# A hybrid attention and convolution trunk on one core: every 1/sqrt moved from VectorE to one GpSimd power instruction

## The chip, the cores and the metric

The kernel runs on one core of a Trainium2 chip. A core has five engines that run side by side, each with its own queue: TensorE (matmuls and transposes, written PE in the profile, with its weight loads as PEld), VectorE (DVE), ScalarE (ACT), GpSimd (POOL) and SyncE (SP, which here only issues DMAs). An instruction starts when it is first in its engine's queue and the semaphores that it waits for have arrived. The metric is the time of one execution on the device in microseconds; for the kernel before it is the median of three runs. One more execution was recorded by the profiler.

## The reference, cut to what matters

Four layers run one after the other on x of 512 tokens by 1024 channels, float32. Layers 0 and 3 are a differential attention (A), layer 1 is a convolution module (B), layer 2 is a latent attention (C). Each begins with an RMS norm and adds its result to x. All that the change touches is the factor 1/sqrt in the norms:

```
def _rms_norm(x, g):
    y = x * lax.rsqrt(jnp.mean(x * x, axis=-1, keepdims=True) + NORM_EPS)
    return y * g
# A: q, k of 8 heads x 2 halves x 64: _rms_norm, then rotary; per head
#    p0 - lam * p1 of two softmaxes, times v; _rms_norm(o, sub_g); * silu(gate); @ w_out
# B: u = a * sigmoid(b); causal depthwise convolution of 31 taps; LayerNorm; silu; * silu(gate); @ w_out
# C: low-rank q and kv, _rms_norm of each latent, of q's and k's parts per head; softmax; * silu(gate); @ w_out
```

## The kernel before, in words

Every float32 matrix product is made of three faster ones: each operand is split into a high part (a cast, mostly on ScalarE) and a low part (a subtraction, on VectorE, in layer 1 on GpSimd). Weights come by DMA in pieces of 256 rows by up to 512 columns (`piece`) into the `raw` buffers (three) and are split into the `w` buffers (four). Activations stand with channels on partitions as X, with Hh and Hl as the split, gain-scaled input of the next layer.

The kernel isn't written in the order in which it runs. A planner (`Plan`) collects every operation as a node with an engine, a cost in microseconds, its readers and writers. `order` then plays the engines against each other with these costs: at each step every engine offers the node that could start first, ties being broken by a priority (the order of writing plus a shift from the table SHIFT, one entry per name and engine), and the node that starts first overall is put next. So the table of shifts and the costs set the order of every engine's queue; the instructions' real durations don't change it. Buffers come from small pools (SLOTS), among them one PSUM buffer `o` in which each head's output is summed.

`rsqrt(v, name)` (line 715) is called at these places:
- `norm_end` (line 864), once per layer, four times: sums of squares of X (made on GpSimd in `norm_block`, tile `L_sqs`) go through a small matmul to `L_ss`, then to the variance `L_v`; the result scales later what the layer's first matmuls gave. Four columns.
- `qk_chunk` in `layer_a` (line 997), four times in layers 0 and 3: 32 columns, result `L_qk_y`.
- `attend_` in `layer_a` (line 1057), once per head, eight times in layers 0 and 3: four columns, result `L_h_or_y`, with which `gate_o` scales the head's output from `o` into V.
- `layer_b`, once: the LayerNorm after the convolution (line 1287), four columns, result `L_lnr_y`, then eight VectorE instructions normalise V, which TensorE transposes (`L_ytr`).
- `layer_c`, once per token tile (three columns, `L_c_y`), and in `q_chunk` (16 columns, `L_q_y`) and `kv_chunk` (8 columns, `L_kv_y`) four times each.

The ten instructions are one group: an integer estimate of the result from the bits of v, then three rounds of Newton's iteration with three instructions each. Nothing of another node comes between them on VectorE. They need a second buffer `_t`.

In layer 1 the convolution is divided: four channel blocks on VectorE (tile `L_c`), two as sums on GpSimd of products that ScalarE makes (`L_cq`, `L_ct`), one on TensorE. The rest of GpSimd's work is the weight splits of layer 1 (`L_ab_w`, `L_g_w`, `L_o_w`), three of layer 0, and the sums of squares.

Of the kernel before, what the change touches and what calls it, by code (L numbers as in the profile page):

```python
# [207 lines left out]
L0_h1_p.dve=1045 L0_h1_sc.dve=265 L0_h1_sc.pe=-311 L0_h1_wt.act=-4 L0_h1_wtr.pe=-292 L0_h2_cf.dve=448
L0_h2_mx.dve=-1387 L0_h2_or_y.dve=2129 L0_h2_osq.act=-1195 L0_h2_oss.dve=-8105 L0_h2_ov.dve=-485 L0_h2_p.act=579
L0_h2_p.dve=-5549 L0_h2_sc.dve=2135 L0_h2_sc.pe=-157 L0_h2_wt.act=-6662 L0_h2_wtr.pe=8 L0_h3_cf.dve=1197  # L210
L0_h3_mx.dve=-11983 L0_h3_or_y.dve=2 L0_h3_osq.act=139 L0_h3_oss.dve=-245 L0_h3_p.act=-4374 L0_h3_p.dve=-517
L0_h3_sc.dve=-1955 L0_h3_sc.pe=1655 L0_h3_wt.act=43 L0_h3_wtr.pe=-193 L0_h4_cf.dve=-1967 L0_h4_mx.dve=4
# [50 lines left out]
L1_yv3.act=365 L1_yv3.dve=1128 L1_yv4.act=-161 L1_yv4.dve=1380 L1_yv5.act=608 L1_yv5.dve=-6 L1_yv6.dve=687
L1_yv7.act=45 L1_yv7.dve=-1903 L2_T.dve=-208 L2_c00_sq.act=23 L2_c00_t.dve=314 L2_c00_y.dve=-1770 L2_c01_sq.act=22
L2_c01_t.dve=-360 L2_c01_v.dve=13054 L2_c01_y.dve=5452 L2_c02_sq.act=3689 L2_c02_t.dve=-1714 L2_c02_v.dve=18723
L2_c02_y.dve=6901 L2_c03_sq.act=-2 L2_c03_t.dve=2 L2_c03_y.dve=-198 L2_c0_a.pe=2275 L2_c0_w.act=2065 L2_c0_w.dve=-447
# [1301 lines left out]
```

## Time and profile before

| | |
|---|---|
| median of 3 runs | 1075.49 us (1072.21 to 1076.08) |
| the profiled execution | 1068.59 us |
| its span, first to last instruction | 1066.7 us |
| TensorE busy | 1012.0 us (95%) |
| VectorE busy | 806.8 us (76%), 2271 instructions |
| ScalarE busy | 642.1 us (60%) |
| GpSimd busy | 209.2 us (20%), 133 instructions |
| mean granted TensorE clock | 0.986 of full speed |

Busy shares overlap, since the engines run side by side. TensorE's matmuls are pipelined and their ends are modelled, so that its busy time is not time at full rate. What counts for the end is where TensorE stands still or another engine is on the chain of work that ended last; an engine that is idle elsewhere costs nothing.

### The profile page before, as it was taken

To read this page: it belongs to the slowest core of one execution; us is meant where nothing else is said; L and a number is where in the kernel's file an instruction comes from. 1 tells how busy PE (TensorE), PEld (TensorE's weight loads), DVE (VectorE), ACT (ScalarE), POOL (GpSimd) and SP (SyncE) were. 2 spreads that over 40 slices of the span, in tenths; PEclk is the share of its full clock that TensorE was granted. 3 is DMA by queue.
4 is the path that set the end of the run, shared out by engine and by line. 5 is a ranking of instruction groups with operands and counts; after the bars stand their busy time and mean duration, and the time that the engine had idled before them with its cause. 6 is when DMAs were issued, how large, how long until landed. Compare 5 with 4: busy or idle time off the path is not lost.

```text
span 1066.7 us, 15176 instructions
## 1 busy us (share of the span) xinstructions
PE 1012.0 (95%) x5089; PEld 840.0 (79%) x5089; DVE 806.8 (76%) x2271; ACT 642.1 (60%) x1351; POOL 209.2 (20%) x133
## 2 busy tenths in 40 slices
PE   7999999998999999995999998999999999999798
PEld 6778877886887887774888777888888788888687
DVE  4764999997755999999256769976573699988871
ACT  6466458658744356895343676754423957667862
POOL 3300000000038599993330000001020000000000
PEclk9999999999999999997999999999999999999899
DMA  8223121220114331302122211112333212312002
GB/s 235 80 70 108 60 80 60 80 83 22 40 41 139 99 99 40 111 17 65 55 94 65 85 49 40 42 36 81 102 95 119 75 58 67 99 40 80 21 21 79
DMA packets 67253, 78.15 MB, mean 73 GB/s; under 512 B 15813, under 2 KB 44741, under 8 KB 67176
## 3 DMA queue, kind: packets, MB, share of 16 engines
q1 hardware_dynamic: 67176, 77.19, 23.8%
q8 instruction: 40, 0.66, 0.3%
q14 instruction: 37, 0.30, 0.1%
HBM read 75.08 MB, written 2.10 MB: 72 GB/s over the span
## 4 chain that ended last, share of the span: by engine, by line
PE 60%; DVE 16%; ACT 12%; issue 5%; POOL 5%; DMA 1%; SPq 1%; DVEq 0%; ACTq 0%; POOLq 0%
PE L_o L451 18%; PE L_g_a L451 12%; PE L_qk_a L451 10%; PE L_v_a L451 6%; ACT L_qk_st L488 3%; DVE L_c L513 3%; POOL L_cq L504 3%; PE L_ab_a L451 2%; POOL L_sqs L504 1%; PE L_c_a L451 1%; ACT G L481 1%; PE L_ytr L457 1%; DVE L_qk_T L501 1%; DVE L_qk_st L501 1%; SPq L545 1%
## 5 line engine op out<-in xcount | busy, mean ns | idle before, releaser
L451 PE MATMUL L_qk_a<-L_qk_w,Hh 128*128 128x512 f32 x512 | 163.0, 399 | 0.5 <-ACT Hh L481 0.5
L451 PE MATMUL L_o<-L_y,L_o_w 128*128 128x512 f32 x576 | 142.5, 398 | 3.0 <-ACT L_y L481 1.7
L504 POOL TENSOR_TENSOR L_sqs<-L_sqs,L_sq 128x512 f32<-128x512 f32 x28 | 43.8, 1564 | 497.3 <-ACT L_sqs L481 264.7
L451 PEld LDWEIGHTS L_o<-L_y,L_o_w 128*128 128x128 f32 x576 | 106.6, 190 | 25.7 <-DVE L_y L513 2.1
L451 PE MATMUL L_g_a<-L_g_w,Hh 128*128 128x512 f32 x384 | 120.1, 394 | 0.3 <-ACT V L481 0.3
L451 PEld LDWEIGHTS L_qk_a<-L_qk_w,Hh 128*128 128x128 f32 x512 | 93.7, 190 | 18.2 <-ACT Hh L481 0.7
L513 DVE SCALAR_TENSOR_TENSOR L_c<-L_u,L_tab,L_c 128x512 f32<-128x512 f32 x150 | 104.2, 743 | 1.0
L451 PE MATMUL L_qk_a<-L_qk_w,Hl 128*128 128x512 f32 x256 | 101.0, 394 | 3.8 <-DVE Hl L513 3.8
L451 PEld LDWEIGHTS L_g_a<-L_g_w,Hh 128*128 128x128 f32 x384 | 70.5, 188 | 15.0 <-ACT V L481 0.9
L451 PE MATMUL L_v_a<-L_v_w,Hh 128*128 128x512 f32 x256 | 81.2, 398 | 0.2 <-ACT V L481 0.2
L451 PE MATMUL L_ab_a<-Hh,L_ab_w 128*128 128x512 f32 x256 | 81.3, 393 | 0.1
L504 POOL TENSOR_TENSOR L_cq<-L_cq,L_ct 128x512 f32<-128x512 f32 x60 | 79.6, 1327 | 5.5 <-ACT L_ct L481 2.1
L451 PE MATMUL L_g_a<-L_g_w,Hl 128*128 128x512 f32 x192 | 75.0, 390 | 0.0
L451 PEld LDWEIGHTS L_qk_a<-L_qk_w,Hl 128*128 128x128 f32 x256 | 48.4, 189 | 15.1 <-DVE Hl L513 4.6
L488 ACT CAST L_qk_st<-L_qk_tr 64x512 fp32r<-64x512 f32 x96 | 55.6, 579 | 4.8 <-PE L_qk_tr L457 3.7
L451 PEld LDWEIGHTS L_ab_a<-Hh,L_ab_w 128*128 128x128 f32 x256 | 48.0, 188 | 11.4 <-DVE L_u L501 1.1
L488 ACT CAST L_g_w<-L_g_w_r 128x1024 fp32r<-128x1024 f32 x32 | 33.6, 1053 | 36.9 <-PE L_v_a L451 23.3
L501 DVE TENSOR_TENSOR L_qk_st<-L_qk_tr,L_qk_st 64x512 fp32r<-64x512 f32 x64 | 44.1, 688 | 15.2 <-ACT L_qk_st L488 13.9
L481 ACT ACTIVATE L_ct<-L_u,L_tab 128x512 f32<-128x512 f32 x60 | 43.2, 721 | 19.8 <-POOL L_cq L504 19.3
L451 PEld LDWEIGHTS L_v_a<-L_v_w,Hh 128*128 128x128 f32 x256 | 46.0, 188 | 9.1 <-ACT V L481 0.4
L501 DVE TENSOR_TENSOR L_qk_w<-L_qk_w_r,L_qk_w 128x1024 fp32r<-128x1024 f32 (+1 forms) x30 | 35.4, 1182 | 22.0 <-ACT L_qk_w L488 21.6
L488 ACT CAST L_qk_w<-L_qk_w_r 128x1024 fp32r<-128x1024 f32 (+1 forms) x33 | 34.0, 1032 | 28.6 <-PE L_g_a L451 18.6
(377 smaller groups left out, 2373.1 us busy)
## 6 DMA issues: line engine op xcount, KB each, us to landing
L_qk_w_r<-a_w_in SPq DMA_DIRECT2D x62, 256.0 KB, 3.0
L_v_w_r<-a_w_in SPq DMA_DIRECT2D x16, 512.0 KB, 4.2
L_g_w_r<-a_w_in SPq DMA_DIRECT2D x16, 512.0 KB, 3.7
L_o_w_r<-a_w_out SPq DMA_DIRECT2D x16, 512.0 KB, 3.5
L_ab_w_r<-b_w_in SPq DMA_DIRECT2D x24, 256.0 KB, 2.9
L_g_w_r<-b_w_in SPq DMA_DIRECT2D x8, 512.0 KB, 3.7
L_o_w_r<-b_w_out SPq DMA_DIRECT2D x8, 512.0 KB, 3.5
L_g_w_r<-c_w_in SPq DMA_DIRECT2D x8, 512.0 KB, 3.7
```

What stands on the lines that cost most here:

```text
L451: lambda nc: nc.tensor.matmul(out.real(), a.real(), b.real(), start=start, stop=stop),
L457: emit = lambda nc: nc.tensor.transpose(out.real(), src.real(), ident.real())
L481: nc.scalar.activation(out.real(), src.real(), func, scale=scale.real() if isinstance(scale, View) else scale, **kw)
L488: lambda nc: nc.scalar.copy(out.real(), src.real()), [src], [out])
L501: lambda nc: nc.vector.tensor_tensor(out=out.real(), in0=a.real(), in1=b.real(), op=op), [a, b], [out])
L504: lambda nc: nc.gpsimd.tensor_tensor(out=out.real(), in0=a.real(), in1=b.real(), op=op), [a, b], [out])
L513: self.add("dve", out.n / 960.0 + (0.13 if isinstance(scalar, View) else 0.068), lambda nc: nc.vector.scalar_tensor_tensor(out=out.real(), ...
L545: lambda nc: q(nc).dma_start(out.real(), src), [], [out], dma=out.n * 4 * parts)
```

## The change

`rsqrt` becomes one GpSimd instruction, v to the power of -0.5, as a tensor_tensor with a constant tile. The constant, 32 columns of -0.5, is set once by VectorE at the start. In the planner the node has a cost of 1.0 us on GpSimd at every width, in place of a VectorE group with the sum of ten instructions' costs and 1.15. The buffer `_t` goes. The table SHIFT is replaced as a whole: 875 entries before, 892 after, 770 names in common, none with the same value; entries of GpSimd are 12 before and 47 after.

```diff
 SHIFT = {k: int(v) for k, v in (x.split("=") for x in """
-L0_g0_a.act=27 L0_g0_a.pe=-118 L0_g0_w.act=560 L0_g0_w.dve=-4872 L0_g0_w_r.sp=8 L0_g1_a.act=-39309 L0_g1_a.pe=1592
...
+L3_y1.dve=-176 L3_y2.act=-5673 L3_y2.dve=-13 L3_y3.act=1884 L3_y3.dve=1217 L3_ytr0.pe=962 L3_ytr1.pe=5075
...
 """.split())}
...
         self.p.memset(self.ones[:, :], 1.0)
+        self.p.memset(self.half[:, :], -0.5)
...
     def rsqrt(self, v, name):
 
-        p = self.p
-        y, t = self.small(v.n, name + "_y"), self.small(v.n, name + "_t")
-        with p.group("dve"):
-            p.ts(y.bitcast(I32), v.bitcast(I32), -0.5, ALU.mult, 1597463007.0, ALU.add)
-            for _ in range(3):
-                p.stt(t, y, -0.5, y, ALU.mult, ALU.mult)
-                p.tt(t, t, v, ALU.mult)
-                p.stt(y, t, 1.5, y, ALU.add, ALU.mult)
-            p.open.cost += 1.15
+        y = self.small(v.n, name + "_y")
+        h = self.half[:, 0:v.n]
+        self.p.add("pool", 1.0, lambda nc: nc.gpsimd.tensor_tensor(
+            out=y.real(), in0=v.real(), in1=h.real(), op=ALU.pow), [v, h], [y])
         return y
...
-    for n, shape, dt in (("ident", [P, P], F32), ("ones", [P, P], F32), ("X", [P, NK, S], F32),
+    for n, shape, dt in (("ident", [P, P], F32), ("ones", [P, P], F32), ("half", [P, 32], F32), ("X", [P, NK, S], F32),
```

## Rows read from the trace of the kernel before

**Rows 1.** The page: busy time by engine; GpSimd's busy tenths in 40 slices.
```profile
PE 1012.0 (95%) x5089; PEld 840.0 (79%) x5089; DVE 806.8 (76%) x2271; ACT 642.1 (60%) x1351; POOL 209.2 (20%) x133
...
POOL 3300000000038599993330000001020000000000
```

**Rows 2.** The page: the chain that ended last, by engine.
```profile
PE 60%; DVE 16%; ACT 12%; issue 5%; POOL 5%; DMA 1%; SPq 1%; DVEq 0%; ACTq 0%; POOLq 0%
```

**Rows 3.** Stretches: length, busy PE, PEld, DVE, ACT, POOL; granted clock, DMA share, GB/s.
```profile
120.00:180.00 60.00, 59.34 (x301) 47.99 (x300) 56.08 (x154) 37.23 (x77) 0.00 (x0) 1.00 0.23 69
...
240.00:300.00 60.00, 54.24 (x300) 44.49 (x299) 44.23 (x173) 44.00 (x115) 0.00 (x0) 0.97 0.09 28
...
480.00:505.00 25.00, 12.13 (x60) 9.44 (x59) 24.49 (x56) 13.04 (x22) 8.54 (x5) 0.73 0.21 69
...
590.00:640.00 50.00, 47.40 (x241) 39.60 (x239) 39.02 (x132) 35.55 (x77) 0.00 (x0) 1.00 0.21 61
640.00:700.00 60.00, 52.80 (x352) 47.66 (x352) 56.20 (x216) 40.50 (x115) 0.00 (x0) 0.97 0.14 45
...
985.00:1030.00 45.00, 37.51 (x201) 30.76 (x200) 37.61 (x149) 34.80 (x84) 0.00 (x0) 0.92 0.04 13
```

**Rows 4.** TensorE's waits: waiter <- releaser: us in total, times, longest.
```profile
PE L_ytr L457 <- ACT L_h5j_p L481: 4.6, 1, 4.6
...
PE L_h2j_wtr L457 <- ACT L_h2j_p L481: 2.6, 1, 2.6
```

**Rows 5.** Timeline 484 to 506: start, us, engine, line, operation [idle before <-releaser].
```profile
484.88 1.31 POOL L504 TENSOR_TENSOR L_cq<-L_cq,L_ct 128x512 f32<-128x512 f32 x1
...
486.24 1.12 PE L457 MATMUL L_ctr<-ident,L_cq 128*128 128x128 f32 x4 [5.60 <-POOL L_cq L504]
...
491.60 0.17 DVE L522 TENSOR_SCALAR L_lnr_y<-L_v 128x4 int32<-128x4 int32 x1
...
493.38 0.16 DVE L513 SCALAR_TENSOR_TENSOR L_lnr_y<-L_lnr_t,L_lnr_y 128x4 f32<-128x4 f32 x1
493.57 3.74 DVE L522 TENSOR_SCALAR V<-V,L_mv,L_lnr_y 128x512 f32<-128x512 f32 x8
...
494.27 4.67 PE L457 MATMUL L_ytr<-ident,V 128*128 128x128 f32 x20 [6.91 <-DVE V L522]
```

**Rows 6.** Timeline of VectorE, 988 to 991: one chain of 32 columns.
```profile
988.54 0.18 DVE L522 TENSOR_SCALAR L_qk_y<-L_qk_v 128x32 int32<-128x32 int32 x1
...
990.56 0.19 DVE L513 SCALAR_TENSOR_TENSOR L_qk_y<-L_qk_t,L_qk_y 128x32 f32<-128x32 f32 x1
```

**Rows 7.** Line 522: count, ns min/median/max, first and last start in us.
```profile
L522 DVE TENSOR_SCALAR L_r_y<-L_v x4: 160/170/1174, 50.4 to 791.5; 128x4 int32<-128x4 int32 x4
...
L522 DVE TENSOR_SCALAR L_kv_y<-L_kv_v x4: 164/168/173, 599.1 to 692.3; 128x8 int32<-128x8 int32 x4
...
L522 DVE TENSOR_SCALAR L_q_y<-L_q_v x4: 166/168/175, 605.6 to 685.9; 128x16 int32<-128x16 int32 x4
```

**Rows 8.** Line 504, GpSimd: the same columns.
```profile
L504 POOL TENSOR_TENSOR L_cq<-L_cq,L_ct x60: 1260/1296/1782, 367.9 to 484.9; 128x512 f32<-128x512 f32 x60
L504 POOL TENSOR_TENSOR L_sqs<-L_sqs,L_sq x28: 1272/1460/2158, 23.4 to 779.2; 128x512 f32<-128x512 f32 x28
...
L504 POOL TENSOR_TENSOR L_o_w<-L_o_w_r,L_o_w x8: 2377/2410/2864, 475.2 to 530.2; 128x1024 fp32r<-128x1024 f32 x8
```

**Rows 9.** Layer 2's tables: line 501 by form, and the chain: start, us, what.
```profile
L501 DVE TENSOR_TENSOR L_tab<-L_setup x18: 277/348/2565, 21.0 to 709.7; 128x128 f32<-128x128 f32 x12, 128x256 f32<-128x256 f32 x6
...
481.98 7.25 DVE L_tab L501 x6
```

**Rows 10.** Stretch 240 to 300, records of the tile L_h_or_t alone: VectorE.
```profile
240.00:300.00 60.00, 5.84 (x36) 0.97 0.09 28
```

**Rows 11.** The chain of waits, 625 to 705: start, us, what.
```profile
654.05 0.19 DVE L_q_y L522
...
658.70 0.47 ACT L_h2j_p L481 x2
```

More of the change, by code (lines that the diff above doesn't have):

```diff
@@ L208 @@
[L208 to L212, printed above, removed]
@@ L263 @@
[L263 to L266, printed above, removed]
-L2_c0_w_r.sp=-5670 L2_g0_a.pe=24924 L2_g0_w.act=-506 L2_g0_w.dve=130 L2_g0_w_r.sp=2796 L2_g1_a.act=1554 L2_g1_a.pe=392
@@ L338 @@
-L3_ytr2.pe=-50 L3_ytr3.pe=-23 L3_ytr4.pe=-2546 L3_ytr5.pe=-630 L3_ytr7.pe=-46 none.act=3426 none.dve=28
+L0_g0_a.act=-3563 L0_g0_a.pe=-1240 L0_g0_w.act=6679 L0_g0_w.dve=-45 L0_g1_a.act=-17044 L0_g1_a.pe=-2 L0_g1_w.act=-2673
+L0_g1_w.dve=4891 L0_h0_cf.dve=196 L0_h0_mx.dve=62 L0_h0_or_y.dve=280 L0_h0_or_y.pool=231 L0_h0_osq.act=8822
+L0_h0_oss.dve=310 L0_h0_ov.dve=-265 L0_h0_p.act=2958 L0_h0_p.dve=214 L0_h0_sc.dve=-217 L0_h0_sc.pe=-1938
+L0_h0_wt.act=-2027 L0_h0_wtr.pe=3135 L0_h1_cf.dve=-231 L0_h1_mx.dve=144 L0_h1_or_y.dve=183 L0_h1_or_y.pool=-1633
@@ new lines @@
+L0_h1_osq.act=1884 L0_h1_oss.dve=5505 L0_h1_ov.dve=-23927 L0_h1_p.act=-2142 L0_h1_p.dve=199 L0_h1_sc.dve=-7
+L0_h1_sc.pe=1482 L0_h1_wtr.pe=-15202 L0_h2_cf.dve=-28 L0_h2_mx.dve=-6468 L0_h2_or_y.dve=7565 L0_h2_osq.act=951
+L0_h2_oss.dve=-4299 L0_h2_ov.dve=2637 L0_h2_p.act=-44448 L0_h2_p.dve=-1247 L0_h2_sc.dve=-26647 L0_h2_sc.pe=-4
+L0_h2_wt.act=-3852 L0_h3_mx.dve=1362 L0_h3_or_y.dve=-297 L0_h3_or_y.pool=-31 L0_h3_osq.act=-4253 L0_h3_ov.dve=819
+L0_h3_p.act=15 L0_h3_p.dve=176 L0_h3_sc.dve=1377 L0_h3_sc.pe=-2546 L0_h3_wt.act=-153 L0_h3_wtr.pe=111
@@ new lines @@
+L0_h6_wt.act=-5174 L0_h6_wtr.pe=-1442 L0_h7_cf.dve=1069 L0_h7_mx.dve=-1 L0_h7_or_y.dve=1186 L0_h7_or_y.pool=-3223
+L0_h7_osq.act=2070 L0_h7_oss.dve=-245 L0_h7_ov.dve=553 L0_h7_p.act=-1465 L0_h7_p.dve=159 L0_h7_sc.dve=-2
+L0_h7_sc.pe=-12 L0_h7_wt.act=102 L0_h7_wtr.pe=-137 L0_lay.act=2013 L0_lay.dve=-7848 L0_o0.pe=-1804 L0_o01.dve=1392
+L0_o01.pe=77 L0_o02.dve=-17861 L0_o02.pe=-811 L0_o03.dve=2420 L0_o03.pe=-75 L0_o0_w.act=14 L0_o0_w.dve=2975
+L0_o0_w_r.sp=-3322 L0_o1.dve=1763 L0_o1.pe=-9320 L0_o10.dve=4099 L0_o10.pe=321 L0_o11.dve=-7541 L0_o11.pe=182
@@ new lines @@
+L0_qk1_st.act=3336 L0_qk1_st.dve=-3316 L0_qk1_t.dve=1 L0_qk1_tr.pe=-1811 L0_qk1_v.dve=2079 L0_qk1_w.act=3870
+L0_qk1_w.dve=-2062 L0_qk1_y.dve=-31 L0_qk2_a.pe=244 L0_qk2_sq.act=619 L0_qk2_ss.dve=-4813 L0_qk2_st.act=4574
+L0_qk2_st.dve=-5 L0_qk2_t.dve=2 L0_qk2_tr.pe=-15 L0_qk2_v.dve=4789 L0_qk2_w.act=14287 L0_qk2_y.dve=-999
+L0_qk2_y.pool=7478 L0_qk3_T.dve=-2835 L0_qk3_a.pe=1002 L0_qk3_sq.act=-6762 L0_qk3_ss.dve=741 L0_qk3_st.act=188
+L0_qk3_st.dve=-1103 L0_qk3_t.dve=307 L0_qk3_tr.pe=-2509 L0_qk3_v.dve=-20325 L0_qk3_w.act=274 L0_qk3_w.dve=-10607
@@ new lines @@
+L0_tr20.act=15 L0_tr20.dve=-2286 L0_tr20.pe=3080 L0_tr24.act=-1196 L0_tr24.dve=-2238 L0_tr24.pe=1472 L0_tr30.act=288
+L0_tr30.dve=-1451 L0_tr30.pe=-405 L0_tr34.act=2592 L0_tr34.dve=332 L0_tr34.pe=280 L0_v.dve=-18577 L0_v0_a.act=45
+L0_v0_a.pe=-4828 L0_v0_w.act=1353 L0_v0_w.dve=-4216 L0_v0_w_r.sp=-285 L0_v1_a.act=-1282 L0_v1_a.pe=1076
+L0_v1_w.act=2766 L0_v1_w.dve=2736 L0_v1_w_r.sp=2657 L0_warm.pe=-7816 L0_x1.sp=492 L0_y0.act=-4856 L0_y0.dve=-225
+L0_y1.act=1684 L0_y1.dve=-6296 L0_y2.act=264 L0_y2.dve=-163 L0_y3.act=1390 L0_y3.dve=2806 L0_ytr1.pe=457
@@ new lines @@
+L1_yv1.dve=-1646 L1_yv2.act=478 L1_yv2.dve=-153 L1_yv3.act=-683 L1_yv3.dve=-5059 L1_yv4.act=-77 L1_yv5.act=5963
+L1_yv5.dve=-1091 L1_yv6.act=-1192 L1_yv6.dve=-2338 L1_yv7.act=-1942 L1_yv7.dve=273 L2_T.act=8677 L2_T.dve=224
+L2_c00_sq.act=89 L2_c00_t.dve=-1284 L2_c00_v.dve=-3125 L2_c00_y.dve=-683 L2_c00_y.pool=8218 L2_c01_sq.act=-718
+L2_c01_t.dve=245 L2_c01_v.dve=17 L2_c01_y.dve=793 L2_c01_y.pool=1042 L2_c02_sq.act=-7 L2_c02_t.dve=1545
+L2_c02_v.dve=-11316 L2_c02_y.dve=-12069 L2_c02_y.pool=135 L2_c03_sq.act=7020 L2_c03_t.dve=-11509 L2_c03_y.dve=571
@@ new lines @@
+L2_c03_y.pool=472 L2_c0_a.pe=-4 L2_c0_w_r.sp=-4750 L2_g0_a.act=-919 L2_g0_a.pe=182 L2_g0_w.act=1011 L2_g0_w.dve=-74
+L2_g0_w_r.sp=-785 L2_g1_a.act=1771 L2_g1_a.pe=-14467 L2_g1_w.act=2348 L2_g1_w.dve=1888 L2_g1_w_r.sp=2643
+L2_h0_mx.dve=167 L2_h0_p.act=883 L2_h0_wt.act=-1115 L2_h0_wtr.pe=-8758 L2_h1_mx.dve=-953 L2_h1_p.act=-1344
+L2_h1_sc.dve=-22 L2_h1_sc.pe=-1333 L2_h1_wt.act=-46 L2_h1_wtr.pe=-12873 L2_h2_mx.dve=-1800 L2_h2_p.act=-5336
+L2_h2_sc.dve=-47 L2_h2_sc.pe=-5910 L2_h2_wt.act=647 L2_h2_wtr.pe=-10004 L2_h3_mx.dve=-1027 L2_h3_p.act=-5
@@ new lines @@
+L2_h3_sc.dve=77 L2_h3_wtr.pe=-458 L2_h4_mx.dve=-4016 L2_h4_p.act=-1430 L2_h4_sc.pe=-623 L2_h4_wt.act=-922
+L2_h4_wtr.pe=-3946 L2_h5_mx.dve=6 L2_h5_p.act=1316 L2_h5_sc.dve=21 L2_h5_sc.pe=-1673 L2_h5_wt.act=1398
+L2_h5_wtr.pe=1475 L2_h6_mx.dve=3095 L2_h6_p.act=3976 L2_h6_sc.dve=-90 L2_h6_sc.pe=-6207 L2_h6_wt.act=-11388
+L2_h6_wtr.pe=-4991 L2_h7_mx.dve=-134 L2_h7_sc.pe=-1185 L2_h7_wt.act=-936 L2_h7_wtr.pe=-209 L2_kv0_T.act=1339
+L2_kv0_T.dve=111 L2_kv0_a.pe=1490 L2_kv0_sq.act=47 L2_kv0_ss.dve=-862 L2_kv0_v.dve=263 L2_kv0_w.act=-4388
@@ new lines @@
+L2_kv0_w.dve=4586 L2_kv0_w_r.sp=11972 L2_kv1_T.act=831 L2_kv1_T.dve=-1882 L2_kv1_a.act=3472 L2_kv1_a.pe=-2007
+L2_kv1_sq.act=582 L2_kv1_ss.dve=4408 L2_kv1_v.dve=701 L2_kv1_w.dve=125 L2_kv1_w_r.sp=4593 L2_kv1_y.pool=9931
+L2_kv2_T.act=-296 L2_kv2_T.dve=716 L2_kv2_a.act=-4922 L2_kv2_a.pe=1100 L2_kv2_sq.act=-2025 L2_kv2_ss.dve=-2820
+L2_kv2_v.dve=-38 L2_kv2_w.act=-572 L2_kv2_w.dve=2040 L2_kv3_T.act=249 L2_kv3_a.act=5509 L2_kv3_a.pe=4
+L2_kv3_sq.act=25406 L2_kv3_ss.dve=-206 L2_kv3_v.dve=470 L2_kv3_w.act=-31 L2_kv3_w.dve=-23904 L2_kv3_w_r.sp=-3
@@ new lines @@
+L2_kv3_y.pool=-4120 L2_l0.dve=1411 L2_l1.dve=7061 L2_l2.dve=1 L2_l3.dve=276 L2_l4.dve=303 L2_l5.dve=42134
+L2_l6.dve=-680 L2_l7.dve=555 L2_lat0.act=-2838 L2_lat1.dve=-8529 L2_lay.act=6960 L2_lay.dve=82 L2_lay.sp=-207
+L2_ltr0.pe=2471 L2_ltr1.pe=824 L2_ltr2.pe=11684 L2_ltr3.pe=-2709 L2_o0.dve=-217 L2_o0.pe=260 L2_o00.dve=-4
+L2_o00.pe=324 L2_o01.dve=-57 L2_o01.pe=131 L2_o02.dve=-46 L2_o02.pe=-1644 L2_o03.dve=54 L2_o03.pe=-451 L2_o0_w.act=-4
+L2_o0_w.dve=-1542 L2_o0_w_r.sp=1125 L2_o1.dve=3493 L2_o1.pe=588 L2_o10.pe=-56 L2_o11.dve=2123 L2_o11.pe=-5220
@@ new lines @@
+L2_o12.pe=-427 L2_o13.dve=-1335 L2_o13.pe=6482 L2_o1_w_r.sp=1027 L2_o2.dve=2500 L2_o3.dve=-4931 L2_o3.pe=-15596
+L2_o4.dve=2906 L2_o4.pe=44053 L2_o5.dve=362 L2_o5.pe=-15 L2_o6.dve=-1056 L2_o6.pe=-1783 L2_o7.dve=-8440 L2_o7.pe=214
+L2_p0_rt.act=-4348 L2_p0_rt.dve=-16 L2_p0_rtr.pe=-5764 L2_p0_st.act=14084 L2_p0_tr.pe=2 L2_p1_rt.act=75
+L2_p1_rt.dve=-645 L2_p1_rtr.pe=21 L2_p1_st.act=-278 L2_p1_st.dve=5679 L2_p1_tr.pe=-21 L2_p2_rt.act=-9
+L2_p2_rt.dve=13965 L2_p2_rtr.pe=289 L2_p2_st.act=-57 L2_p2_st.dve=-3776 L2_p2_tr.pe=1823 L2_p3_rt.act=-17355
@@ new lines @@
+L3_h7_or_y.dve=-1201 L3_h7_or_y.pool=1502 L3_h7_osq.act=-3 L3_h7_oss.dve=-1757 L3_h7_ov.dve=6404 L3_h7_p.act=118
+L3_h7_p.dve=11809 L3_h7_sc.dve=-1361 L3_h7_wt.act=-2249 L3_h7_wtr.pe=1521 L3_lay.act=1348 L3_lay.dve=-3889
+L3_lay.sp=1396 L3_o0.dve=-4885 L3_o00.pe=-204 L3_o01.pe=3093 L3_o02.pe=2413 L3_o03.pe=977 L3_o0_w.act=163
+L3_o0_w.dve=987 L3_o0_w_r.sp=-19724 L3_o1.dve=-1373 L3_o1.pe=123 L3_o10.pe=670 L3_o11.pe=3441 L3_o12.pe=-2347
+L3_o130.pe=7734 L3_o131.pe=8550 L3_o1_w.act=4236 L3_o1_w_r.sp=17041 L3_o2.dve=971 L3_o2.pe=-1144 L3_o3.dve=886
@@ new lines @@
+L3_o4.dve=-269 L3_o4.pe=-14 L3_o5.dve=-909 L3_o5.pe=4169 L3_o6.pe=66 L3_o7.dve=-13256 L3_o7.pe=-1835 L3_ot000.act=1923
+L3_ot000.sp=-2525 L3_ot010.act=15 L3_ot010.sp=2238 L3_ot020.sp=-11579 L3_ot030.act=297 L3_ot030.sp=-19755
+L3_ot100.act=15 L3_ot110.act=264 L3_ot110.sp=-43 L3_ot120.act=-2638 L3_ot120.sp=-205 L3_ot130.act=-2046
+L3_ot130.sp=1150 L3_ot13256.act=-519 L3_ot13256.sp=3066 L3_qk0_a.pe=400 L3_qk0_sq.act=-1200 L3_qk0_st.act=-23
+L3_qk0_t.dve=-889 L3_qk0_tr.pe=880 L3_qk0_v.dve=249 L3_qk0_w.act=1585 L3_qk0_w.dve=1527 L3_qk0_w_r.sp=-84
@@ new lines @@
+L3_qk3_w.act=788 L3_qk3_w.dve=10369 L3_qk3_w_r.sp=-4 L3_qk3_y.dve=-49 L3_qk3_y.pool=3280 L3_r10.dve=42
+L3_r11.dve=-1883 L3_r13.dve=-59 L3_r14.dve=77 L3_r15.dve=218 L3_r16.dve=16604 L3_r17.dve=-4153 L3_r_y.pool=1030
+L3_rq.dve=275 L3_setup.dve=-4577 L3_setup.sp=381 L3_sq1.act=3356 L3_sq2.act=-21 L3_sq4.act=14467 L3_sq5.act=111
+L3_sq6.act=1269 L3_sq7.act=47 L3_sqs.act=1753 L3_sqs.pool=4017 L3_ss.pe=2046 L3_tab.dve=-111 L3_v.dve=-448
+L3_v0_a.act=-49 L3_v0_a.pe=-1723 L3_v0_w.act=-48 L3_v0_w.dve=-35 L3_v0_w_r.sp=-841 L3_v1_a.act=-620 L3_v1_w.act=-971
@@ L339 @@
+L3_v1_w.dve=4248 L3_v1_w_r.sp=6300 L3_y0.act=-49 L3_y0.dve=13627 L3_y1.act=12395 L3_y1.dve=867 L3_y2.act=-857
+L3_y2.dve=4399 L3_y3.act=3190 L3_y3.dve=12 L3_ytr0.pe=-44 L3_ytr1.pe=489 L3_ytr2.pe=1783 L3_ytr3.pe=25 L3_ytr4.pe=-309
+L3_ytr5.pe=-4022 L3_ytr6.pe=-2057 L3_ytr7.pe=3 none.act=-1474 none.dve=1165
 """.split())}
```

188 lines of the change are left out of this document (65 added, 123 removed).

## The prediction

> **What bounds the kernel now.** I read the page's busy line first: TensorE is busy 1012.0 of 1066.7 us, VectorE 806.8, GpSimd 209.2 [rows 1]. So 54.7 us are all the idle TensorE time there is, and work that leaves VectorE pays only where TensorE waits for it. The chain of waits says that such places exist: a quarter of it runs over VectorE and ScalarE [rows 2]. The table by stretch says where. Taking TensorE's busy time from each stretch's length: 0.7 us idle in 120-180, although VectorE is busy 56.08 of 60 there; 5.8 in 240-300 (last heads of layer 0), 12.9 in 480-505 (end of layer 1's convolution, LayerNorm), 2.6 in 590-640 and 7.2 in 640-700 (attention of layer 2), 7.5 in 985-1030 (last heads of layer 3) [rows 3]. That is 36 us; the rest is the start, the end and small pieces. The list of TensorE's waits names the releasers: ScalarE's exponentials once for 4.6 us and once for 2.6 [rows 4]; in the timeline VectorE's normalised V for 6.91 and GpSimd's last convolution sum for 5.60 [rows 5].
>
> **What the change removes.** There are 41 calls of rsqrt: four norms at the layers' heads, one LayerNorm, 12 in each of the two A layers (4 query/key chunks, 8 heads), 12 in layer 2. The 25 calls of 3 or 4 columns run like the LayerNorm's: from 491.60 to 493.54, 1.94 us for ten instructions [rows 5]. The 8 calls of 32 columns run from 988.54 to 990.75, 2.21 us [rows 6]. For the 8 of 8 and 16 columns I take 2.02, between the two. VectorE loses 25 x 1.94 + 8 x 2.21 + 8 x 2.02 = 48.5 + 17.7 + 16.2 = 82.4 us of its queue, and 1.0 more where one first instruction took 1174 ns in place of 170 [rows 7]. In busy time that is 410 instructions of about 0.17 us, 70 us: 806.8 should become about 737. The memset of the constant, 32 columns once at the start, has no wait behind it; I count nothing (a short VectorE instruction is 0.16 us [rows 5]).
>
> **What it adds.** 41 GpSimd instructions. No row shows a power. Below it is bounded by GpSimd's addition: 1296 ns for 512 columns and 2410 for 1024 [rows 8] make 2.18 ns a column and 0.18 us fixed, so 0.19 us for 4 columns and 0.25 for 32. Above, I let the longest undisturbed GpSimd row stand, 2.4 us. The small ones are nearest in shape to the low end, but a power is many steps per element; I take 0.7, between the ends by ratio, and keep 0.2 to 2.4. The code's planner charges 1.0 for every width. Two handovers, VectorE to GpSimd and back, come on top: I take 0.15 together, a little over twice the 0.05 us between GpSimd's last convolution sum, ended at 486.19, and TensorE's transpose of it at 486.24 [rows 5]. So 0.85 us from variance to result in place of 1.94, bounds 0.35 and 2.55.
>
> The added wait is on VectorE: the instruction that uses the result (r times rs, or V times r) stands in its queue, and what is behind it waits too. The planner fills the gap for 1.0 us plus handovers; as long as a power takes less, VectorE stands still only where it has nothing else, as at the LayerNorm.
>
> GpSimd's slices show no work in most of layers 0, 2 and 3 [rows 1], so the heads' and chunks' powers meet an empty queue. In layer 1 they don't: eight weight splits of 2.4 us stand there from 475.2 to 530.2 [rows 8].
>
> A shared resource: VectorE and GpSimd disturb each other. A GpSimd sum of 1272 ns at best took up to 2158 [rows 8], a VectorE table product of 348 ns up to 2565 [rows 9], and the held instruction of [rows 7] belongs to the same kind. I take this at nothing on the path, since it costs VectorE at most the power's 0.7 us out of the 2.0 freed; its upper bound is 41 x 0.7 = 29 us of VectorE. The Trainium skill (SBUF — State Buffer, "Who interferes with whom") says that a VectorE instruction with two SBUF inputs and a GpSimd instruction that reads SBUF exclude each other for a whole instruction; the trace agrees, with the 2565 ns above. By that rule in its hardest form every power would take its length from VectorE, 54 of 83 us would stay freed, and the gain below would shrink in proportion, from 9 to 6 us.
>
> **What of it is on the path.**
> - 480-505: the LayerNorm's chain stands bare between V's variance and the V that TensorE waits for [rows 5]: 1.94 - 0.85 = 1.1 us.
> - 240-300: four of the chains lie here (36 records, nine to a chain [rows 10]), 7.8 us of VectorE against 5.8 us of TensorE idle, with ScalarE as busy as VectorE (44.00 against 44.23 [rows 3]). I take 2, a third.
> - 590-700: all eight q and kv chains, by their first and last starts [rows 7], 16 us of VectorE against 9.8 idle. One is plainly the cause: the q chain from 654.05 to about 656.1, then V, then the exponential at 658.70 for which TensorE waited 2.6 us [rows 4, 11]. In 640-700 VectorE (56.20) is well busier than ScalarE (40.50); I take 4.
> - 985-1030: the 4.6 us wait is ScalarE's own queue; I take 1.
> - Clock: 0.73 granted in 480-505 and 0.92 in 985-1030 [rows 3]; that is 6.75 and 3.6 us worth of full clock, TensorE dropping to the lower of its two levels after it had idled. Shorter waits give perhaps 1 back.
> - 120-240, 830-985 and the norms between layers: nothing, TensorE's own matmuls are the cover. If that cover were gone, each chain would cost its 0.85 us.
>
> Sum: 1.1 + 2 + 4 + 1 + 1 = 9 us. Next to be late are ScalarE in the attention tails and GpSimd's convolution at 486. Against the profiled execution, 1068.59 us, that gives about 1059.6; that execution is 6.9 us below the median of the three timed runs, 1075.49, so on their scale, 9 us lower, I forecast 1066.
>
> **The new table** reorders everything (892 entries, none of the 770 common names keeps its value). What such an order can gain or lose is seen at 480-494: from 475 on, weight splits of 2.4 us stand inside GpSimd's chain of sums [rows 8], and layer 2's tables stand for 7.25 us on VectorE, stretched from 348 ns each, ahead of the statistics that the LayerNorm needs [rows 9]. Nothing in the trace says where the new order puts them. I take zero for it, and plus or minus 8.
>
> **Rivals.**
> 1. *Relief and a better seam.* Forecast, and the 7 us of tables or one or two splits no longer ahead of LayerNorm, with 4 of the 6.75 us of clock back: 1066 - 7 - 4 = 1055. For: the size of that wait. Against: the seam is a matter of order, not of rsqrt.
> 2. *Hidden.* TensorE is 95% busy and ScalarE ends much of its waiting [rows 4]; VectorE just idles more: 1075, within 0.5%. For: 120-180 with VectorE full and TensorE not waiting.
> 3. *The power is dear.* VectorE is relieved of 2.03 us per call (83.4 over 41) minus what the power takes beyond the planner's 1.0. With the gain in proportion, at my upper bound of 2.4 it is 3 us (1072), at 3.0 us nil, and at 5 us 9 us are lost: 1084. It decides from 3.0 us on. Against: no GpSimd row of even 1024 columns is that long undisturbed.
> 4. *LayerNorm's power queued behind splits (slower).* Place: GpSimd's queue after 475. Each split put ahead of the power costs 2.4 us bare [rows 8], and the waits for the splits' own inputs on top. With three of them ahead, 7.2 us, another drop of the clock as dear as that in 985-1030 (3.6), and only 2 us of relief elsewhere: 7.2 + 3.6 - 2 = +8.8, some 1084. With so little relief it decides from the first split on, with all of the 8 us elsewhere from the fourth; the same length lost at another seam through the new order counts here too.
>
> **Chances.** Forecast 0.40, rival 1 0.15, rival 2 0.22, rival 3 0.08, rival 4 0.15. Half a per cent, 5.4 us, is about what a measurement of this kernel tells from no change. The forecast case spreads over 1059 to 1073 and gives 0.34 faster and 0.06 same; rival 1 is faster; rival 2 same; of 3 and 4 0.02 fall within the bound. Faster 0.49, same 0.30, slower 0.21. The forecast's own range is 1059 to 1073; to hold 8 in 10 it must reach rival 1 with some room and the two slow cases: 1048 to 1084.
>
> **What would show it.** Power rows of 0.2 to 1 us, about as long for 32 columns as for 4; VectorE near 1860 instructions and 737 us, GpSimd at 174 and about 240 us; TensorE's idle time down to about 46 us, the loss mostly in 590-700; V after the LayerNorm's variance within 1 us. It is wrong if a power takes over 2.4 us, if VectorE shows idle time that GpSimd ends in most chains, if TensorE's idle time stays, or if the largest difference lies at the end of the convolution and comes from the order.

## The result: 0.9% slower

The changed kernel takes 1082.24 us (median of 8 runs, 1081.49 to 1085.62) against 1073.24 for the kernel before beside it (8 runs, 1067.83 to 1076.08). The ratio is 1.0093, with a 95% interval of 1.0068 to 1.0118. The loss is small but clear of the noise. The forecast was 1066, 9 us under the kernel before, so even the sign was wrong. The profiled execution took 1082.88 us; its mean granted clock was 0.979 of full speed, where the one before had 0.986.

From the page of the kernel after: span, busy time by engine, GpSimd's busy tenths in 40 slices, the chain that ended last.

```profile
span 1081.0 us, 14821 instructions
...
PE 1016.5 (94%) x5089; PEld 840.3 (78%) x5089; DVE 741.7 (69%) x1862; ACT 640.5 (59%) x1351; POOL 294.3 (27%) x174
...
POOL 2410112020047499993521111100320020202000
...
PE 56%; DVE 13%; ACT 12%; POOL 10%; issue 6%; DMA 1%; SPq 1%; POOLq 0%; ACTq 0%; DVEq 0%
```

VectorE lost 65.1 us of work [rows 1], near the 70 of the forecast. But GpSimd gained 85.1, and its share of the chain that ended last doubled from 5% to 10% [rows 2]: by line, the wide powers are 3% of it, and the convolution's sums went from 3% to 5%. TensorE stands idle for 64.5 us (1081.0 - 1016.5), where it had been 54.7. The powers themselves say why. This is the line that issues them, by tile: count, ns min/median/max, first and last start, shapes.

```profile
L722 POOL TENSOR_TENSOR L_h_or_y<-L_h_ov,half x16: 1007/1007/1377, 156.5 to 1054.9; 128x4 f32<-128x4 f32 x16
...
L722 POOL TENSOR_TENSOR L_qk_y<-L_qk_v,half x8: 5427/5616/6345, 53.0 to 980.0; 128x32 f32<-128x32 f32 x8
...
L722 POOL TENSOR_TENSOR L_c_y<-L_c_v,half x4: 850/854/1713, 568.4 to 576.7; 128x3 f32<-128x3 f32 x4
L722 POOL TENSOR_TENSOR L_kv_y<-L_kv_v,half x4: 1637/1637/1639, 608.6 to 706.9; 128x8 f32<-128x8 f32 x4
L722 POOL TENSOR_TENSOR L_q_y<-L_q_v,half x4: 2900/2902/2932, 610.2 to 689.7; 128x16 f32<-128x16 f32 x4
...
L722 POOL TENSOR_TENSOR L_lnr_y<-L_v,half x1: 1027/1027/1027, 498.6 to 498.6; 128x4 f32<-128x4 f32 x1
```

The shortest times, 850, 1007, 1637, 2900 and 5427 ns for 3, 4, 8, 16 and 32 columns, lie on a line of about 0.38 us and 0.157 us a column ((5427 - 1007) / 28 = 158 ns). The plan charges 1.0 for each, which fits the narrow calls of 3 and 4 columns alone. A query/key chunk takes five and a half times its planned time, where the ten instructions on VectorE took 2.21 us [rows 6].

Who pays is in VectorE's waits for the powers: waiter, releaser, us in total, times, longest.

```profile
DVE L_qk_y L503 <- POOL L_qk_y L722: 29.0, 8, 5.3
...
DVE L_h_or_y L503 <- POOL L_h_or_y L722: 4.1, 6, 1.1
DVE L_q_y L524 <- POOL L_q_y L722: 3.7, 3, 1.9
DVE L_kv_T L503 <- POOL L_kv_y L722: 3.0, 4, 1.8
```

All eight chunks hold VectorE, 29.0 us together. Three of them reach TensorE with a long wait:

```profile
PE L_ctr L459 <- POOL L_cq L506: 8.2, 1, 8.2
PE L_qk_tr L459 <- DVE L_qk_T L503: 6.0, 2, 4.8
PE L_qk_tr L459 <- DVE L_qk_st L503: 5.2, 2, 5.0
PE L_ytr L459 <- DVE V L524: 4.1, 1, 4.1
...
PE L_v_a L453 <- DVE L_v_w L503: 2.9, 1, 2.9
```

The second, the third and the last row are new. How they come about is seen in the timeline of one chunk in layer 0 and two in layer 3 (start, us, engine, line, operation, in brackets the idle time before it and who ended it): GpSimd, VectorE and TensorE from 131 to 139, from 884 to 898, and from 976 to 992.

```profile
131.43 1.22 DVE L503 TENSOR_TENSOR L_v_w<-L_v_w_r,L_v_w 128x1024 fp32r<-128x1024 f32 x1
131.60 6.34 POOL L722 TENSOR_TENSOR L_qk_y<-L_qk_v,half 128x32 f32<-128x32 f32 x1 [73.21 <-DVE L_qk_v L524]
...
137.97 0.19 DVE L503 TENSOR_TENSOR L_qk_y<-L_qk_y,L_lay 128x32 f32<-128x32 f32 x1 [5.32 <-POOL L_qk_y L722]
...
138.84 2.24 PE L459 MATMUL L_qk_tr<-ident,L_qk_T 128*128 128x128 f32 x8 [4.80 <-DVE L_qk_T L503]
...
885.53 0.69 DVE L503 TENSOR_TENSOR L_qk_T<-L_qk_T,L_qk_t 128x512 f32<-128x512 f32 x1
885.71 5.80 POOL L722 TENSOR_TENSOR L_qk_y<-L_qk_v,half 128x32 f32<-128x32 f32 x1 [39.43 <-DVE L_qk_v L524]
...
891.54 0.19 DVE L503 TENSOR_TENSOR L_qk_y<-L_qk_y,L_lay 128x32 f32<-128x32 f32 x1 [3.89 <-POOL L_qk_y L722]
891.65 1.22 DVE L503 TENSOR_TENSOR L_v_w<-L_v_w_r,L_v_w 128x1024 fp32r<-128x1024 f32 x1
...
892.92 0.80 PE L453 MATMUL L_v_a<-L_v_w,Hh 128*128 128x512 f32 x1 [2.93 <-DVE L_v_w L503]
...
979.83 1.21 DVE L503 TENSOR_TENSOR L_g_w<-L_g_w_r,L_g_w 128x1024 fp32r<-128x1024 f32 x1
...
979.99 6.34 POOL L722 TENSOR_TENSOR L_qk_y<-L_qk_v,half 128x32 f32<-128x32 f32 x1 [22.18 <-DVE L_h5j_mx L503]
...
986.37 0.19 DVE L503 TENSOR_TENSOR L_qk_y<-L_qk_y,L_lay 128x32 f32<-128x32 f32 x1 [5.19 <-POOL L_qk_y L722]
986.59 0.68 DVE L503 TENSOR_TENSOR L_qk_st<-L_qk_tr,L_qk_st 64x512 fp32r<-64x512 f32 x1
...
989.69 1.09 PE L459 MATMUL L_qk_tr<-ident,L_qk_T 128*128 128x128 f32 x4 [4.98 <-DVE L_qk_st L503]
```

At 891.54 the multiplication by rs waits 3.89 us for the power. The weight split behind it, which has no use for the power, waits with it, and TensorE stands still for that split. At 986.37 the same befalls a `L_qk_st` of transposes made earlier. At 138.84 TensorE waits 4.80 us for what is scaled with the result itself, `L_qk_T`. Together that is 4.80 + 2.93 + 4.98 = 12.7 us.

Each of the three waits is followed by a stretch in which the granted clock fell to the lower of its two levels. Stretches of the kernel after: length, busy PE, PEld, DVE, ACT, POOL; granted clock, DMA share, GB/s.

```profile
138.80:146.00 7.20, 7.16 (x23) 5.73 (x24) 4.65 (x8) 4.50 (x8) 0.00 (x0) 0.60 0.25 75
...
889.00:897.00 8.00, 5.07 (x19) 3.97 (x18) 4.77 (x15) 0.68 (x2) 3.51 (x2) 0.69 0.36 123
897.00:900.00 3.00, 3.00 (x11) 2.40 (x11) 1.25 (x2) 2.93 (x6) 0.00 (x0) 0.69 0.00 0
...
987.00:995.00 8.00, 5.31 (x18) 4.47 (x19) 7.77 (x14) 6.87 (x12) 0.00 (x0) 0.57 0.20 64
```

In work at full clock that is 7.2 x 0.40 + 11 x 0.31 + 8 x 0.43 = 9.7 us. Part of it is counted among the waits already: near 892.0 and 987.6 the clock had fallen while TensorE still stood idle (granted clock 0.51 in 892 to 893, 0.79 in 987 to 988), for some 3.0 us, worth 1.5. So the clock took about 8.2 us from the work, and waits and clock make some 20.9 us.

### The profile page after: what moved, and what is told of

Same layout as the page of the kernel before. It is cut to its first block, busy times and chain, and to the rows that moved or that the text cites. A ratio compares the mean times of both kernels' runs of the same rounds, so it can differ in the third digit from the quotient of the medians.

```text
span 1081.0 us, 14821 instructions
## 1 busy us (share of the span) xinstructions
PE 1016.5 (94%) x5089; PEld 840.3 (78%) x5089; DVE 741.7 (69%) x1862; ACT 640.5 (59%) x1351; POOL 294.3 (27%) x174
## 4 chain that ended last, share of the span: by engine, by line
PE 56%; DVE 13%; ACT 12%; POOL 10%; issue 6%; DMA 1%; SPq 1%; POOLq 0%; ACTq 0%; DVEq 0%
PE L_o L453 17%; PE L_qk_a L453 13%; PE L_g_a L453 9%; PE L_v_a L453 5%; POOL L_cq L506 5%; POOL L_qk_y L722 3%; ACT L_qk_st L490 2%; PE L_c_a L453 2%; DVE L_c L515 1%; DVE L_qk_T L503 1%; PE L_ab_a L453 1%; ACT G L483 1%; ACT L_ct L483 1%; PE L_qk_tr L459 1%; DVE L_qk_st L503 1%
## 5 line engine op out<-in xcount | busy, mean ns | idle before, releaser
L453 PE MATMUL L_qk_a<-L_qk_w,Hh 128*128 128x512 f32 x512 | 165.6, 405 | 1.3 <-POOL L_qk_w L506 1.3
L453 PEld LDWEIGHTS L_o<-L_y,L_o_w 128*128 128x128 f32 x576 | 105.7, 188 | 23.2 <-POOL L_o_w L506 0.9
L722 POOL TENSOR_TENSOR L_qk_y<-L_qk_v,half 128x32 f32<-128x32 f32 x8 | 46.1, 5758 | 211.9 <-DVE L_qk_v L524 189.7
L722 POOL TENSOR_TENSOR L_h_or_y<-L_h_ov,half 128x4 f32<-128x4 f32 x16 | 16.6, 1040 | 245.6 <-DVE L_h_ov L524 130.4
L506 POOL TENSOR_TENSOR L_sqs<-L_sqs,L_sq 128x512 f32<-128x512 f32 x28 | 39.7, 1418 | 84.4 <-ACT L_sqs L483 56.4
L503 DVE TENSOR_TENSOR L_qk_st<-L_qk_tr,L_qk_st 64x512 fp32r<-64x512 f32 x64 | 44.1, 689 | 19.1 <-ACT L_qk_st L490 17.7
```

The costliest lines, as they stand in the source:

```text
L453: lambda nc: nc.tensor.matmul(out.real(), a.real(), b.real(), start=start, stop=stop),
L503: lambda nc: nc.vector.tensor_tensor(out=out.real(), in0=a.real(), in1=b.real(), op=op), [a, b], [out])
L506: lambda nc: nc.gpsimd.tensor_tensor(out=out.real(), in0=a.real(), in1=b.real(), op=op), [a, b], [out])
L722: self.p.add("pool", 1.0, lambda nc: nc.gpsimd.tensor_tensor(out=y.real(), in0=v.real(), in1=h.real(), op=ALU.pow), [v, h], [y])
```

## The experiments

In the expectations D is the theory that the wide powers, 5.6 us long but planned at 1.0, cost the time; O is the theory that the new order of the work costs it, whatever the powers take; T, in the two runs that name it, is the theory that a power costs only where it outlasts the matmuls that TensorE has at hand. Other letters are rivals for their own run. Times are medians; each ratio is to the kernel before, run on the same chip.

**Cheap powers in the same order.** The first of these makes the eight 32-column powers a multiplication by a constant; the second does so for all 41. The records of each engine stand in the same order as in the kernel after, but for one more short instruction that sets a constant; so they do in the two later runs that halve or repeat powers, the added powers aside.

```diff
...
-            out=y.real(), in0=v.real(), in1=h.real(), op=ALU.pow), [v, h], [y])
+            out=y.real(), in0=v.real(), in1=h.real(), op=ALU.mult if cheap else ALU.pow), [v, h], [y])
```

> The order of every queue is that of the changed kernel; only the eight powers of 32 columns become multiplications by a constant (their results are not 1/sqrt, so this part of the computation is left out). Theory D (dear power: the 32-column powers of 5.6 us hold VectorE's queue and with it TensorE's transposes, because the planner charged 1.0): GpSimd's eight instructions fall to 0.2 to 0.4 us, VectorE's 29.0 us of waiting for them to under 3, TensorE's 11.2 us of waiting before L_qk_tr to under 2, and the time by 8 to 13 us below the changed kernel: 1069 to 1074, ratio to before 0.996 to 1.001. Theory O (the new order is worse by itself, at the start and the end of the convolution): at most 3 us below the changed kernel, ratio 1.006 to 1.009.

> As e1, with all 41 powers as multiplications (no 1/sqrt is computed anywhere). Theory D: the powers of 16 and 8 columns (2.9 and 1.6 us) cost a little too, those of 3 and 4 columns (1.0 us, as the planner charges) nothing: 1 to 4 us below e1, ratio 0.992 to 0.999. Theory O: as e1, ratio 1.005 to 1.009. If the time lies clearly under the kernel before, the change would have paid with a power as cheap as an addition.

Measured: 1059.61 us (ratio 0.9872, 0.9852 to 0.9893) and 1056.22 (0.9853, 0.9829 to 0.9878). With the eight wide ones cheap, 22.6 us go and the kernel is faster than before; the other 33 are worth 3.4 more. That leaves no room for O, which allowed 3 us; D had the direction and the waits, but its 8 to 13 us were about half of the gain. From the first of these kernels, the multiplication that stands for a power:

```profile
L724 POOL TENSOR_TENSOR L_qk_y<-L_qk_v,half x8: 252/440/1169, 54.6 to 962.6; 128x32 f32<-128x32 f32 x8
```

The stretches around the three waits, in the kernel after (first three rows) and with cheap wide powers (last three):

```profile
120.00:180.00 60.00, 52.90 (x263) 43.12 (x263) 48.16 (x137) 36.66 (x84) 13.14 (x3) 0.94 0.20 62
830.00:900.00 70.00, 67.03 (x324) 55.28 (x323) 45.31 (x117) 40.52 (x82) 7.81 (x3) 0.95 0.22 68
985.00:1045.00 60.00, 51.99 (x277) 42.92 (x277) 43.70 (x135) 43.01 (x98) 4.51 (x4) 0.94 0.14 45
...
120.00:180.00 60.00, 57.98 (x299) 47.54 (x299) 55.65 (x163) 42.17 (x98) 3.80 (x4) 1.00 0.23 71
830.00:900.00 70.00, 69.49 (x340) 57.00 (x339) 51.78 (x142) 44.03 (x88) 2.64 (x3) 1.00 0.23 68
985.00:1045.00 60.00, 56.17 (x309) 45.88 (x309) 33.01 (x114) 31.83 (x84) 3.02 (x3) 1.00 0.10 32
```

VectorE has no wait for `L_qk_y` left, TensorE none for `L_qk_tr`, and the clock is full where it had dropped. The spans differ by 1081.0 - 1057.8 = 23.2 us. Of these 15.0 are TensorE's idle time (64.5 against 1057.8 - 1008.3 = 49.5) and 8.2 its busy time (1016.5 against 1008.3), the same 5089 matmuls at a mean clock of 0.979 against 0.990; the account above found 12.7 and 8.2. The 8.2 us for the convolution's sum stay, so they aren't the wide powers' doing.

**Each table with the other form.** One kernel takes the new table with the ten VectorE instructions, the other the old table with the powers (its values for the nodes that moved from VectorE to GpSimd moved with them). In the first kernel the new table's values for these nodes stand under GpSimd's name and apply to nothing, so that it isn't quite the new order.

```diff
 SHIFT = {k: int(v) for k, v in (x.split("=") for x in """
-(the kernel's own table)
+(the other kernel's table)
```

> The kernel before with the new table of priorities: ten VectorE instructions per rsqrt, no power. Theory D: the table alone isn't the loss; but it was made for other nodes, so some loss is possible: 1070 to 1080, ratio 0.997 to 1.006. Theory O: at least as slow as the changed kernel: 1080 to 1095, ratio 1.006 to 1.02.

> The changed kernel with the old table (each rsqrt node, now on GpSimd, keeps the old shift of its name). Theory D: the powers are as long here, VectorE waits about 25 to 35 us for the 32-column ones, and the time is 1078 to 1095, ratio 1.005 to 1.02. Theory O: with the old order the loss goes: 1065 to 1075, ratio 0.993 to 1.002.

Measured: 1183.50 us (1.1028, 1.1002 to 1.1054) and 1125.62 (1.0485, 1.0460 to 1.0511). Both are far above what either theory gave. In the second, VectorE still waits 23.9 us for the wide powers; but before against after had made a difference of 9 us, and this one of 52. So a table is worth something only with the costs that it was made for, and a swap of tables can't separate the two parts of this change. In the first, TensorE stands idle for 114.5 us (1182.0 - 1067.5) at a mean clock of 0.942, spread over many waits of which the longest is 6.8 us; no single cause is shown.

**Half as wide.** 16 of the 32 columns by power, the rest by multiplication; same order, same planned cost.

```diff
...
+            nc.gpsimd.tensor_tensor(out=y[:, 0:w].real(), in0=v[:, 0:w].real(), in1=g[:, 0:w].real(), op=ALU.pow)
+            if w < v.n:
+                nc.gpsimd.tensor_tensor(out=y[:, w:32].real(), in0=v[:, w:32].real(), in1=g[:, 32:48].real(), op=ALU.mult)
```

> The changed kernel's order again; of each 32-column power only 16 columns are a power, the others a multiplication by a constant (half of these results are not 1/sqrt). The wide call should take 2.9 + 0.3 = 3.2 us, between e1's 0.4 and the changed kernel's 5.6. Theory D in its plain form, each us beyond the planner's 1.0 has the same price: (3.2 - 0.4) / (5.6 - 0.4) = 54% of the way from 1059.6 to 1082.2: 1071 to 1073, ratio to before 0.997 to 1.000. Theory T (a threshold: TensorE has matmuls for some us, and stalls, with its clock dropping, only when the power outlasts them): under a quarter of the way, 1060 to 1065, ratio 0.987 to 0.992.

Measured: 1068.15 us (0.9974, 0.9958 to 0.9990), 8.5 above the cheap kernel. By the times that is 38% of the way; by the ratios, each to the kernel before on its own chip (1071.03 here, 1073.87 there), it is 46%. T's quarter is out. D's 54% isn't: the time lies under its range, the ratio within it. VectorE's wait shows what a power costs more closely than its length does:

```profile
DVE L_qk_y L503 <- POOL L_qk_y L728: 11.5, 6, 3.0
```

11.5 of 29.0 us are 40%. Work at hand covers about the same part of each power, 5.6 - 29.0 / 8 = 2.0 us of the whole one and 3.3 - 11.5 / 8 = 1.9 of the half one, and what sticks out costs. Per microsecond of this wait the loss is 8.5 / 11.5 = 0.74 here and 22.6 / 29.0 = 0.78 with the whole power by the times, 0.95 and 0.82 by the ratios.

**Narrow powers twice.** Each power of 3 or 4 columns is issued twice, 25 us more on GpSimd, none of them wide.

```diff
...
+            for _ in range(2 if v.n <= 4 else 1):
+                nc.gpsimd.tensor_tensor(out=y.real(), in0=v.real(), in1=h.real(), op=ALU.pow)
```

> The changed kernel's order; every power of 3 or 4 columns is run twice, 2.0 in place of 1.0 us for 25 calls (a doubled cost, nothing left out). Theory D: what overruns the planner's 1.0 costs wherever it stands, at e1's price of 22.6 us for 8 x 5.2 us, 0.54 us per us: 25 us more make +13 us, 1095, ratio 1.020. Theory T: 1 us is covered by TensorE's matmuls nearly everywhere but at the LayerNorm: +1 to +4 us, 1083 to 1087, ratio 1.009 to 1.013.

Measured: 1098.18 us (1.0250, 1.0219 to 1.0282), 15.9 above the kernel after, where D gave 13 and T 1 to 4. VectorE's waits there:

```profile
DVE L_qk_y L503 <- POOL L_qk_y L725: 29.1, 8, 5.3
DVE L_h_or_y L503 <- POOL L_h_or_y L725: 17.2, 15, 2.2
...
DVE L_c_y L524 <- POOL L_c_y L725: 4.7, 4, 1.7
```

The heads' wait grew from 4.1 us to 17.2. So a narrow power that outruns its plan costs as well, not the wide ones alone. T, by which a narrow power of 2 us is covered nearly everywhere, falls here.

**The true cost in the plan.** The node gets 0.38 + 0.157 us a column in place of 1.0: first with the table of the kernel after, then with a table searched for these costs.

```diff
-        self.p.add("pool", 1.0, lambda nc: nc.gpsimd.tensor_tensor(
+        self.p.add("pool", 0.38 + 0.157 * v.n, lambda nc: nc.gpsimd.tensor_tensor(
```

> The changed kernel with one constant corrected: the planner charges a power 0.38 + 0.157 us a column, as its rows in the changed kernel show, in place of 1.0; the table is that of the changed kernel, not searched again. Rival P (the right price alone mends it): 1055 to 1065, near e1. Theory D with what e3 and e4 showed (a table serves only the costs that it was searched with): slower than the changed kernel, 1090 to 1125, ratio 1.015 to 1.05.

> As e7, with the table searched for this price (a random search of some 250,000 orders in the planner, the best one kept). Theory D (the wrong price was the loss, the power itself pays): under the kernel before by more than e1, 1045 to 1060, ratio 0.975 to 0.988. Rival W (a 32-column power, 5.6 us against 2.2 on VectorE, is too long for any order): 1070 or more, ratio 0.997 or more.

Measured: 1116.08 us (1.0395, 1.0374 to 1.0415) and 1047.85 (0.9764, 0.9744 to 0.9784). The true cost alone cuts VectorE's wait for the wide powers from 29.0 to 7.6 us, and the kernel is still slower than the one after: P is out. With the true cost and its own table the kernel beats both: 2.4% under before, about 3% under after (1047.85 / 1082.24 = 0.968). Its page, its wide powers, VectorE's wait for them, and one chunk of layer 3 on GpSimd and VectorE:

```profile
span 1045.2 us, 14805 instructions
...
PE 1003.9 (96%) x5089; PEld 835.5 (80%) x5089; DVE 744.1 (71%) x1862; ACT 642.3 (61%) x1351; POOL 297.2 (28%) x174
```

```profile
L728 POOL TENSOR_TENSOR L_qk_y<-L_qk_v,half x8: 5426/5430/6335, 49.5 to 947.4; 128x32 f32<-128x32 f32 x8
```

```profile
DVE L_qk_y L509 <- POOL L_qk_y L728: 5.6, 5, 1.4
```

```profile
947.45 5.74 POOL L728 TENSOR_TENSOR L_qk_y<-L_qk_v,half 128x32 f32<-128x32 f32 x1 [20.55 <-DVE L_qk_v L530]
...
950.88 0.68 DVE L509 TENSOR_TENSOR L_qk_T<-L_qk_T,L_qk_t 128x512 f32<-128x512 f32 x1
...
952.24 0.55 DVE L535 TENSOR_REDUCE L_h5j_mx<-L_h5j_sc 128x1 f32<-128x384 f32 x1
953.22 0.19 DVE L509 TENSOR_TENSOR L_qk_y<-L_qk_y,L_lay 128x32 f32<-128x32 f32 x1 [0.44 <-POOL L_qk_y L728]
```

The powers are as long as in the kernel after, and GpSimd and VectorE are as busy. But the order now puts other work ahead of the instruction that needs the result, and VectorE's wait is 5.6 us in place of 29.0. W is out: the power isn't too slow for this kernel, given an order that has room for it.

**What is the search's and what the powers'.** One control leaves the calls of over 8 columns on VectorE and searches a table for that; the other is the kernel before with its table searched further.

```diff
+        if v.n > 8:
+            p = self.p
+            y, t = self.small(v.n, name + "_y"), self.small(v.n, name + "_t")
...
+            return y
```

> Powers only for calls of up to 8 columns (29 of 41, at the true price); the 16- and 32-column calls keep the ten VectorE instructions; table searched as in e8. Theory D: near e8, within 8 us of it, 1047 to 1062, since VectorE gets back 8 x 2.2 + 4 x 2.1 = 26 us of the 83. Rival W: at least 10 us faster than e8.

> A control: the kernel before, with its ten VectorE instructions, and its own table searched further in the same way. If the search is all that e8 and e9 gain, this one is within 5 us of them; by theory D it gains 3 to 8 us on the kernel before, 1063 to 1069, ratio 0.992 to 0.997, and stays at least 6 us behind e8.

Measured: 1055.75 us (0.9839, 0.9818 to 0.9860) and 1069.96 (0.9972, 0.9959 to 0.9985). On the kernel before the search alone gives 0.3%, a little less than D's 3 to 8 us. Moving the calls of up to 8 columns gives most of the gain, and moving the 16- and 32-column ones too about 8 us more. How much of those 8 us is the luck of one search isn't settled: each table was searched once. Nor was the kernel after searched further at its planned 1.0. The kernel with the true cost and its own table is 8.4 us faster than the one with all 41 powers cheap in the order of the kernel after (1047.85 against 1056.22), though its powers are long; so at least that part of its lead over the kernel after comes from a better order at large, and not from waits for powers. How the rest divides between the right cost and more searching is not shown.

## Why the prediction was wrong, step by step

- **The failed step: "I take 0.7", "between the ends", with bounds of 0.2 to 2.4, and "about as long for 32 columns as for 4".** I bounded a power by GpSimd's addition and by its longest row, and let the fixed part decide. Measured: 0.85 to 1.03 us for the 25 narrow calls, save three that VectorE held up (at most 1.71), above 0.7 but close to the plan's 1.0; 1.64 and 2.90 for the four each of 8 and 16 columns; 5.62 for the eight wide ones, over twice my upper bound. A row of 1024 columns says nothing of an operation that costs 0.157 us a column; addition costs 0.0022 [rows 8]. GpSimd's busy time shows it too: 294.3 us, where I forecast about 240.
- **Rival 3, "the power is dear", was nearest to what happened, at a chance of 0.08.** It priced a call of 5 us at 1084. But it reckoned with a mean over 41 calls, and that mean is only (294.3 - 209.2) / 41 = 2.1 us, below its turning point of 3.0. What decides is each call's excess over its planned time, and who stands behind it. The eight wide calls carry 22.6 us of loss. That 1082.24 comes close to this rival's 1084, to rival 4's 1084 and inside the outer range of 1048 to 1084 is luck: the mean stayed under rival 3's turning point, LayerNorm's power stood in no queue, and the forecast's own range, 1059 to 1073, missed.
- **"as long as a power takes less, VectorE stands still only where it has nothing else"** named the right mechanism: above 1.0 us VectorE stood still in all eight chunks. I didn't work out what stands behind it there: weight splits and stacks that need no power.
- **The chunks in 120-240 and 830-985 I priced at nothing, with "TensorE's own matmuls" as cover, and 0.85 us each without it.** Two of the three long waits lie in those stretches, at 138.8 and 892.9; the third is at 989.7.
- **The relief, 9 us, is there, as far as rows can show it.** In the kernel after, TensorE's idle time in layer 2 fell from 9.8 us (590 to 700) to 5.0 (600 to 710), and in 240 to 300 from 5.8 to 3.4; the sum had 4 and 2 for these. With cheap wide powers the kernel gains 14.3 us on the kernel before beside it (1073.87), with all of them cheap 17.7; that is relief and new order together, and no run divides them. VectorE's 1862 instructions and 741.7 us are as forecast (1860, 737).
- **LayerNorm (rival 4)** came to nothing: its power took 1.03 us at 498.6, after GpSimd had stood idle for 3.5 us. TensorE's wait for V fell from 6.9 us to 4.1, but that for the convolution's sum grew from 5.6 to 8.2 [rows 5], so the seam gained nothing.
- **The disturbance of VectorE by GpSimd, bounded by 29 us, was taken at nothing.** By the hardest form of the rule in the Trainium skill (SBUF — State Buffer, "Who interferes with whom") a power would lock VectorE's two-input instructions out for its whole length. The trace doesn't bear that out: the product at 950.88, with both inputs in SBUF, began 3.4 us into a power of 5.74 and took 0.68 us, as the others of its kind do (671 to 694 ns). The other way round it does: a power waits for a VectorE instruction with two SBUF inputs that is already running. Behind the three long waits this made the powers 0.91, 0.37 and 0.91 us longer (6.34, 5.80 and 6.34 against 5.43), so the disturbance was on the path after all, with up to 2.2 us.
- **The table, "I take zero", plus or minus 8.** With cheap powers the new order and the relief gain together. But an order isn't a term of its own: put together with other costs, a table cost 10% and 5% here, and 4% even with the costs mended.

So the measured +9 us is about -14.3 (relief and new order) and +22.6 (the wide powers' overrun). Both come from the one run with cheap wide powers, so that their sum is no check of either; the idle and busy time of TensorE above are one for the overrun.

## What to carry to other kernels

Before an operation gets a cost in a plan, time it at every width in which it occurs; a neighbour on the same engine says little about an operation of another kind. On an engine that takes its queue in order, an operation that outruns its plan delays everything behind the instruction that waits for it: here 0.7 to 0.95 us for each microsecond of VectorE's wait, where TensorE had little slack, and about a third of that was its clock (8.2 of 23.2 us). When a cost changes, search the order anew before judging the edit: the same powers were 0.9% slower than before in one order and 2.4% faster in the other.
